# First modulations in fp32 on four column groups, and the Hyena filter steps moved into the opening, in a Trainium2 transformer block

## The chip, the cores and the metric

The kernel runs on one core of one Trainium2 chip. The time is that of one execution on the device, in microseconds. The kernel before took 2386.2 us, the median of three runs (2375.78 to 2389.0 us). The profile that is read here is of one more execution, of 2394.28 us.

## What is computed

One block of a diffusion model: 256 latent tokens and 256 context tokens of 2048 channels. The parts that the change touches are the first modulation and the Hyena filters.

```python
mod_c = silu(c_ctx) @ w_ada[:, :2 * D] + b_ada[:2 * D]      # context: shift, scale
mod   = silu(c) @ w_ada + b_ada                             # latents: six parts
parts = modulate(x, shift, scale) @ w_in                    # x * (1 + scale) + shift
hid = sin(sin(feats @ w1 + b1) @ w2 + b2)                   # 256 x 64
h   = (hid @ w3).reshape(L, 2, 2, 1024) * window            # taps: order, direction, channel
kf  = rfft(concat(h_fwd, 0, h_bwd[:0:-1]), n=2 * L)         # spectra of the filters
```

The spectra depend on weights alone; the long convolutions use them in the Hyena branch, much later in the program.

## The kernel before

All large products are made of fp32r matmuls, one pass over the moving operand each, from operands that were split into a high and a low part: `split` casts the high part on ScalarE (L138) and subtracts on VectorE (L139), and three matmuls (high by high, low by high, high by low) make one product. A scheduler orders the instructions of each engine at build time by a modelled time line; each engine then runs its list in that order. A tile waits for a free buffer of its tag ("wraw", "k8" and so on), and a DMA of SP's queue that waits holds up those behind it.

**The opening** has four rounds, q = 0 to 3. Each makes 512 columns of the first two modulations (shift and scale, `part`) for both streams. The silu of the two conditioning vectors, high and low parts, stands in four columns, repeated 32 times over to 128 columns (`csw`). 2048 x 512 of `w_ada` come in as four loads of 1 MB (`load4`), each is split in two pieces of 128x1024 (`split_ring`), and for each of 16 blocks of 128 rows two matmuls of 128 columns by 512 run (L396 with the high part, L397 with the low part). `mod_columns` then copies four rows out of PSUM, turns them into columns by matmuls with `sel` (L374) and adds the bias. `modulated` transposes a block of the inputs (L171) and applies shift and scale (L365), and `keys` and `gates_in` multiply the result by columns of `w_in` (`cm_block`, L220 to L223). These steps stand in a list, `later`, and are interleaved with the matmuls of the next round. Two steps of the filter generator (its two sines, L257 to L265) are in that list as well.

**The value stage** follows in `dn_early`, after the queries: four blocks of `proj_cm_ctx`, each 192 fp32r matmuls, and after each block two steps of the filter generator (`next(filt)`), eight in all. A step loads a window and two weights, makes the taps with four fp32 matmuls of 64 rows (L281), multiplies and adds them on VectorE (L282 to L290), splits them, runs 30 fp32r matmuls of 256 columns for the transform (`dft_mm`, L237 to L239), and stores a spectrum. All of that is one piece of the program, and the transform of a step stands directly behind its taps.

PSUM is used as two tags of four banks; ring, pages ("k8", seven of 8 KB a partition) and slots are SBUF buffers.

Of the kernel before, what the change touches and what calls it, by code (L numbers as in the profile page):

```python
# [16 lines left out]
P = 128  # L17
D = 2048
# [62 lines left out]
def tile_block(ctx: ExitStack, tc: tile.TileContext, A: dict, out: bass.AP):  # L81
# [51 lines left out]
    def bc(ap, shape):  # L133
        return ap.to_broadcast(shape)
# [57 lines left out]
    def as_rows(ap):  # L192
# [13 lines left out]
    nc.vector.tensor_copy(out=csw.rearrange("p k (r c) -> p k r c", c=4),  # L206
                          in_=bc(cs4.bitcast(F32).unsqueeze(2), [P, KT, 32, 4]))
    sel = cst.tile([4, 2], F32, name="sel")
    tt_(out=sel, in0=ident[0:4, 0:2], in1=ident[0:4, 2:4], op=ADD)

# [30 lines left out]
    def filters():  # L241
# [27 lines left out]
        load_const("dft", 2, 512, dh, dl)  # L269
        for c4 in range(4):  # L270
            hf, cs = c4 // 2, slice(c4 * 256, (c4 + 1) * 256)
            hs = slice((c4 % 2) * 256, (c4 % 2 + 1) * 256)
            for o in range(2):
                win, w3a, w3b, ht = page("win", (2, 256), (256,), (256,), (2, 2, 256))
                dma(out=win, in_=A["window"][:, cs].rearrange("(k p) c -> p k c", p=P))
                for d, w3 in enumerate((w3a, w3b)):
                    c0 = (o * 2 + d) * W + c4 * 256
                    dma(out=w3[:64, :], in_=A["hy_filt_w3"][0][:, c0:c0 + 256])
                    ps = sc_ps()
                    for i in range(2):  # L280
                        mm(ps[:, i * 256:(i + 1) * 256], hid[:, i * P:(i + 1) * P], w3[:64, :], start=True, stop=True)  # L281
                    tt_(out=ht[:, d], in0=ps.rearrange("p (i c) -> p i c", i=2), in1=win, op=MUL)  # L282
                hf_, hb_ = ht[:, 0], ht[:, 1]
                sk = slot([1, 256], "k1", "sk")
                dma(out=sk, in_=A["hy_skip"][0][o:o + 1, cs])
                tt_(out=hf_[0:1, 0, :], in0=hf_[0:1, 0, :], in1=sk, op=ADD)
                nc.vector.memset(hb_[0:1, 0, :], 0.0)
                smdf, sp = page("smdf", (2, 2, 256), (4, 256))
                tt_(out=smdf[:, 0], in0=hf_, in1=hb_, op=ADD)
                tt_(out=smdf[:, 1], in0=hf_, in1=hb_, op=SUB)  # L290
                h_, l_ = page("shl", (2, 2, 256), (2, 2, 256), dt=F32R)
                split(smdf, h_, l_)
                for i2 in range(2):
                    ps = sc_ps()
                    for i in range(2):
                        dft_mm(ps[:, i * 256:(i + 1) * 256], dh, dl, 2 * i2 + i, h_[:, i2], l_[:, i2])
                    copy(out=sp[:, 2 * i2:2 * i2 + 2, :].rearrange("p a c -> p (a c)"), in_=ps)
                ps = sc_ps()
                dft_mm(ps[:, 0:256], dh, dl, 2, h_[:, 0], l_[:, 0])
                ny = slot([1, 256], "k1", "ny")  # L300
                copy(out=ny, in_=ps[0:1, 0:256])
                nc.vector.memset(sp[0:1, 2, :], 0.0)
                dma(out=spec[o][hf][:, :, hs], in_=sp)
                dma(out=nyq[o][hf][:, hs], in_=ny)
                yield

# [7 lines left out]
    x_in, c_in = A["x"][0], A["ctx"][0]  # L314
    ring = slot([P, 4, 1024], "m16", "ring", F32R)
    turn = [0]
    raws = {}

    def load4(ap, k0, c0):
        raw = page("raw", (4, 512))  # L320
        nc.sync.dma_start(out=raw, in_=ap[k0 * P:(k0 + 4) * P, c0:c0 + 512].rearrange("(k p) c -> p k c", p=P))
        return raw

    def split_ring(raw):

        n = turn[0]
        turn[0] += 1
        hi = ring[:, n % 4].rearrange("p (k c) -> p k c", k=2)
        lo = slot([P, 2, 512], ("whi", "wlo")[n % 2], "wlo", F32R)
        split(raw, hi, lo)  # L330
        return hi, lo

# [4 lines left out]
    def gates_in(k0):  # L337
        raw, wh, wl = [slot([P, 4, P], "wraw", "wg", t) for t in (F32, F32R, F32R)]
        nc.sync.dma_start(out=raw, in_=w_in[k0 * P:(k0 + 4) * P, C_AB:C_AB + P].rearrange("(k p) c -> p k c", p=P))
        split(raw, wh, wl)  # L340
        for k in range(4):
            kt = k0 + k
            cm_block(pga, wh, wl, 0, k, [(slice(0, T), uxh[:, kt, :], uxl[:, kt, :]),
                                         (slice(T, 2 * T), uch[:, kt, :], ucl[:, kt, :])], kt == 0, kt == KT - 1)

    def keys(k0):
        if k0 % 4 == 0:
            raws["k"] = load4(w_in, k0, C_DK)
        wh, wl = split_ring(raws["k"][:, k0 % 4:k0 % 4 + 2, :])
# [19 lines left out]
    def mod_columns(mod, part, pmod, q):  # L369

        row = slot([4, 512], "k2", "modrow")
        copy(out=row, in_=pmod[0:4, :])
        for cc in range(4):
# [5 lines left out]

    later = []  # L380
    for q in range(4):
# [6 lines left out]
        for part in range(2):  # L388
            pmod = sc_ps()
            for kb in range(8):  # L390
                if kb % 2 == 0:
                    raw = load4(w_ada, kb * 2, part * D + q * 512)
                wh, wl = split_ring(raw[:, (kb % 2) * 2:(kb % 2) * 2 + 2, :])
                for k in range(2):
                    kt = kb * 2 + k
                    mm(pmod, csw[:, kt, :], wh[:, k, :], start=(kt == 0), stop=False)  # L396
                    mm(pmod, csw[:, kt, :], wl[:, k, :], start=False, stop=(kt == KT - 1))  # L397
                if later and (part * 8 + kb) % 2 == 1:
                    later.pop(0)()
            later.insert(0, lambda mod=mod, part=part, pmod=pmod, q=q: mod_columns(mod, part, pmod, q))  # L400
        for cc in range(4):
# [247 lines left out]
    def dn_early():  # L649
# [41 lines left out]
        for blk in range(4):  # L691
            pss = proj_cm_ctx(C_DV + blk * 256)
            for ch in range(2):
# [854 lines left out]
```

## Time and profile before

| what | value |
|---|---|
| median of three runs | 2386.2 us |
| the profiled execution | 2394.28 us |
| its span | 2392.6 us |
| TensorE busy | 2296.5 us, 96% |
| VectorE, ScalarE, GpSimd busy | 68%, 44%, 7% |
| mean granted TensorE clock | 0.986 of 2.4 GHz |
| DMA | 510.97 MB, 214 GB/s over the span |

The profiler shows one execution: for each engine the instructions with their start and duration, and what ended the idle time ahead of them. A matmul's record holds its way through the array, so records of a dense stream overlap; how fast the stream runs is read from the distance of two starts. Rates of the clock are shares of full speed (1.00 is 2.4 GHz, 0.5 is 1.2 GHz).

### The profile page before, as it was taken

To read this page: it belongs to the slowest core of one execution; us is meant where nothing else is said; L and a number is where in the kernel's file an instruction comes from. 1 tells how busy PE (TensorE), PEld (TensorE's weight loads), DVE (VectorE), ACT (ScalarE), POOL (GpSimd) and SP (SyncE) were. 2 spreads that over 40 slices of the span, in tenths; PEclk is the share of its full clock that TensorE was granted. 3 is DMA by queue.
4 is the path that set the end of the run, shared out by engine and by line. 5 is a ranking of instruction groups with operands and counts; after the bars stand their busy time and mean duration, and the time that the engine had idled before them with its cause. 6 is when DMAs were issued, how large, how long until landed. Compare 5 with 4: busy or idle time off the path is not lost.

```text
span 2392.6 us, 37188 instructions
## 1 busy us (share of the span) xinstructions
PE 2296.5 (96%) x14769; PEld 2073.8 (87%) x14769; DVE 1623.4 (68%) x2135; ACT 1052.1 (44%) x1417; POOL 175.0 (7%) x290
## 2 busy tenths in 40 slices
PE   6999898999999999899999999998999999999998
PEld 4889898889899999887888878888978987988986
DVE  6776467877788898976566656666655655555557
ACT  6665434434333433535443444444434433443442
POOL 0000221100200000121110021000000000000000
PEclk9999999999999999999999999999999999999999
DMA  9957767777663323499776797674667777656664
GB/s 324 330 188 256 221 184 239 244 254 240 201 176 96 109 89 107 137 245 276 228 233 215 257 319 254 235 239 129 217 215 231 255 229 231 184 193 224 192 202 149
DMA packets 295851, 510.97 MB, mean 214 GB/s; under 512 B 17414, under 2 KB 155105, under 8 KB 293084
## 3 DMA queue, kind: packets, MB, share of 16 engines
q1 hardware_dynamic: 271488, 422.63, 55.3%
q0 software_dynamic: 21408, 81.48, 10.8%
q10 hardware_dynamic: 2780, 4.47, 0.5%
q8 instruction: 116, 1.90, 0.3%
q14 instruction: 59, 0.48, 0.1%
HBM read 474.07 MB, written 34.45 MB: 213 GB/s over the span
## 4 chain that ended last, share of the span: by engine, by line
PE 68%; DMA 7%; DVE 5%; issue 3%; ACT 1%; POOL 0%; DVEq 0%; SPq 0%; ACTq 0%; POOLq 0%
PE mm L223 8%; PE mm L221 8%; PE mm L220 8%; PE mm L482 7%; PE mm L483 7%; PE mm L481 7%; DMA aw<-in_w_ada_dram 4%; PE mm L807 4%; PE mm L808 3%; PE mm L806 3%; DVE wlo L139 2%; PE ps L1037 1%; PE mm L941 1%; PE mm L942 1%; PE mm L939 1%
## 5 line engine op out<-in xcount | busy, mean ns | idle before, releaser
L138 ACT CAST whi<-wraw 128x1024 fp32r<-128x1024 f32 x584 | 612.9, 1051 | 965.4 <-PE mm L221 271.2
L139 DVE TENSOR_TENSOR wlo<-wraw,whi 128x1024 fp32r<-128x1024 f32 x584 | 708.5, 1221 | 337.7 <-PE mm L223 97.0
L523 DVE SCALAR_TENSOR_TENSOR acc<-aw,csil,acc 128x1024 f32<-128x1024 f32 x120 | 153.8, 1282 | 216.7 <-DMA aw<-in_w_ada_dram 216.4
L223 PE MATMUL mm<-uxh,wlo 128*128 128x256 f32 x1024 | 294.0, 288 | 3.6 <-DVE wlo L139 3.5
L223 PE MATMUL mm<-u2h,wlo 128*128 128x256 f32 x1024 | 291.0, 284 | 0.9 <-DVE wlo L139 0.8
L220 PE MATMUL mm<-u2h,whi 128*128 128x256 f32 x1024 | 290.8, 284 | 0.6 <-ACT u2h L138 0.6
L221 PE MATMUL mm<-u2l,whi 128*128 128x256 f32 x1024 | 290.8, 284 | 0.1
L220 PE MATMUL mm<-uxh,whi 128*128 128x256 f32 x960 | 276.0, 288 | 11.2 <-DVE cy L497 11.2
L221 PE MATMUL mm<-uxl,whi 128*128 128x256 f32 x960 | 275.9, 287 | 0.0
L223 PEld LDWEIGHTS mm<-uxh,wlo 128*128 128x128 f32 x1024 | 199.5, 195 | 5.5 <-DVE wlo L139 4.7
L482 PE MATMUL mm<-wlo,h 128*128 128x512 f32 x480 | 188.4, 393 | 13.7 <-DVE wlo L139 13.5
L223 PEld LDWEIGHTS mm<-u2h,wlo 128*128 128x128 f32 x1024 | 197.4, 193 | 1.3 <-DVE wlo L139 1.3
L220 PEld LDWEIGHTS mm<-u2h,whi 128*128 128x128 f32 x1024 | 197.5, 193 | 1.1 <-ACT u2h L138 1.0
L221 PEld LDWEIGHTS mm<-u2l,whi 128*128 128x128 f32 x1024 | 197.4, 193 | 0.6 <-DVE u2l L139 0.4
L220 PEld LDWEIGHTS mm<-uxh,whi 128*128 128x128 f32 x960 | 187.2, 195 | 11.9 <-issue 11.2
L221 PEld LDWEIGHTS mm<-uxl,whi 128*128 128x128 f32 x960 | 187.1, 195 | 2.0 <-issue 2.0
L483 PE MATMUL mm<-whi,h 128*128 128x512 f32 x480 | 187.4, 390 | 0.0
L481 PE MATMUL mm<-whi,h 128*128 128x512 f32 x480 | 186.9, 391 | 0.0
L807 PE MATMUL mm<-wlo,uxh 128*128 128x512 f32 x384 | 152.7, 398 | 6.1 <-DVE wlo L139 6.1
L808 PE MATMUL mm<-whi,uxl 128*128 128x512 f32 x384 | 152.1, 396 | 0.0
L806 PE MATMUL mm<-whi,uxh 128*128 128x512 f32 x384 | 150.0, 400 | 0.6 <-ACT whi L138 0.6
L223 PE MATMUL mm<-uch,wlo 128*128 128x256 f32 x448 | 127.9, 287 | 0.0
(541 smaller groups left out, 4681.9 us busy)
## 6 DMA issues: line engine op xcount, KB each, us to landing
wraw<-in_w_in_dram SPq DMA_DIRECT2D x264, 512.0 KB, 4.7
wraw<-in_w_ff_dram SPq DMA_DIRECT2D x256, 512.0 KB, 4.0
aw<-in_w_ada_dram SPq DMA_DIRECT2D x128, 512.0 KB, 4.6
raw<-in_w_ada_dram SPq DMA_DIRECT2D x32, 1024.0 KB, 7.9
wraw<-in_w_branch_dram SPq DMA_DIRECT2D x48, 512.0 KB, 5.1
wraw<-in_w_out_dram SPq DMA_DIRECT2D x32, 512.0 KB, 4.4
g_d<-gate POOLq DMA_DIRECT2D x24, 256.0 KB, 4.7
gatel<-g_d POOLq DMA_DIRECT2D x24, 256.0 KB, 5.6
```

The source lines that it names most:

```text
L138: copy(out=hi, in_=src)
L139: tt_(out=lo, in0=src, in1=hi.bitcast(F32), op=SUB)
L220: mm(ps[:, sl], wh[:, k, cs], ah, start=first and i == 0, stop=False, skip_group_check=True)
L221: mm(ps[:, sl], wh[:, k, cs], al, start=False, stop=False, skip_group_check=True)
L223: mm(ps[:, sl], wl[:, k, cs], ah, start=False, stop=last, skip_group_check=True)
L481: mm(pss[i], a, wh[:, k, :], start=(kt == 0), stop=False)
L482: mm(pss[i], a, wl[:, k, :], start=False, stop=False)
L483: mm(pss[i], b, wh[:, k, :], start=False, stop=(kt == nk - 1))
L523: stt(out=acc, in0=a, scalar=csil[:, 0, kt:kt + 1], in1=acc, op0=MUL, op1=ADD)
L806: mm(pg[i], a, wh[:, k, :], start=(kt == 0), stop=False)
L807: mm(pg[i], a, wl[:, k, :], start=False, stop=False)
L808: mm(pg[i], c, wh[:, k, :], start=False, stop=(kt == KT - 1))
```

## The change

1. The modulations are no longer split. `cs32` holds the silu of the two vectors in fp32, in the first two of 32 columns, the other 30 are zero. For each load of 1 MB four fp32 matmuls run, one for each of its four row blocks, each with 32 stationary columns and its own 32 partitions of one PSUM bank (L403). The column matmuls with `sel` then add the four groups, over 128 rows in place of four.
2. `ring` holds two raw loads in place of four high parts; `keys` and `gates_in` load through the same `wload` as all later products.
3. The filter generator has a step for its loads, one for its taps and one for its transform; one call to `next(filt)` runs the loads of step n + 1, the transform of step n - 1 and the taps of step n. Buffers of other tags are used for them.
4. All eleven calls are in the opening: five in the first round, two in each of the other three. The eight calls of the value stage are gone, and those of the sines too.

```diff
-    cs4 = slot([P, KT, 4], "k1", "cs4", F32R)
-    split(csil.rearrange("p a k -> p k a"), cs4[:, :, 0:2], cs4[:, :, 2:4])
-    csw = page("csw", (KT, P), dt=F32R)
...
+    cs32 = slot([P, KT, 32], "k4", "cs32")
+    nc.vector.memset(cs32, 0.0)
+    nc.vector.tensor_copy(out=cs32[:, :, 0:2], in_=csil.rearrange("p a k -> p k a"))
...
+        which = [(c4, o) for c4 in range(4) for o in range(2)]
+        got, made = loads(*which[0]), None
+        for n in range(len(which) + 1):
+            ahead = loads(*which[n + 1]) if n + 1 < len(which) else None
+            if made is not None:
+                spectrum(*which[n - 1], *made)
+            made = taps(*got) if got is not None else None
+            got = ahead
+            yield
...
-    ring = slot([P, 4, 1024], "m16", "ring", F32R)
+    ring = slot([P, 2, 4, 512], "m16", "ring")
...
+    later = [lambda: next(filt) for _ in range(5)]
...
-            for kb in range(8):
-                if kb % 2 == 0:
-                    raw = load4(w_ada, kb * 2, part * D + q * 512)
-                wh, wl = split_ring(raw[:, (kb % 2) * 2:(kb % 2) * 2 + 2, :])
-                for k in range(2):
-                    kt = kb * 2 + k
-                    mm(pmod, csw[:, kt, :], wh[:, k, :], start=(kt == 0), stop=False)
-                    mm(pmod, csw[:, kt, :], wl[:, k, :], start=False, stop=(kt == KT - 1))
-                if later and (part * 8 + kb) % 2 == 1:
+            for kb in range(4):
+                raw = load_ada(4 * kb, part * D + q * 512)
+                for j in range(4):
+                    mm(pmod[32 * j:32 * j + 32, :], cs32[:, 4 * kb + j, :], raw[:, j, :],
+                       start=(kb == 0), stop=(kb == 3))
+                for _ in range(-(-len(later) // (8 - 4 * part - kb))):
                     later.pop(0)()
...
-        if q in (1, 2):
-            later.append(lambda: next(filt))
+        if q < 3:
+            later += [lambda: next(filt) for _ in range(2)]
...
-            next(filt)
-            next(filt)
```

**How the orders move.** TensorE at the program's start, first before and then in the change (`ps` is a PSUM bank, `ring` and `wlo` are the high and low parts before, `ring` and `raw` the raw loads in the change):

```order
L171 MATMUL ps_75<-idon,colA_rows_68 128x128
L396 MATMUL ps_112<-ring_102,csw_83 128x512
L397 MATMUL ps_112<-wlo_115,csw_83 128x512
L396 MATMUL ps_112<-ring_102,csw_83 128x512
L397 MATMUL ps_112<-wlo_115,csw_83 128x512
```

```order
L171 MATMUL ps_75<-idon,colA_rows_68 128x128
L403 MATMUL ps_112<-ring_102,cs_3_80 32x512 x4
L258 MATMUL ps_127<-fT_118,w_18_120 64x256
L403 MATMUL ps_112<-raw_139,cs_3_80 32x512 x4
L403 MATMUL ps_112<-ring_102,cs_3_80 32x512 x4
L258 MATMUL ps_145<-z_129,w_19_122 64x256
L288 MATMUL ps_182<-w_30_168,z_147 128x256 x2
L288 MATMUL ps_186<-w_30_168,z_147 128x256 x2
L238 MATMUL ps_212<-shl_195,dfts_162 128x256
L238 MATMUL ps_226<-shl_195,dfts_162 128x256
```

Thirty-two matmuls of 512 columns for one modulation of a round became sixteen, in groups of four; three groups, the two sines and the first taps now stand ahead of the first transform, and the fourth group behind it.

TensorE in the value stage, before, around the taps of the third filter step (`vy` and `mm` belong to the values, `win` to the taps, `shl` and `dfts` to the transform), and in the change around the same transposes of values:

```order
L237 MATMUL ps_2442<-shl_2411,dfts_2387 128x256
L238 MATMUL ps_2442<-shl_2411,dfts_2387 128x256
L239 MATMUL ps_2442<-shl_2411,dfts_2387 128x256
L281 MATMUL ps_2457<-win_2454,z_1273 128x256 x2
L223 MATMUL mm_2902<-uch_100,wlo_3083 128x256
L220 MATMUL mm_2902<-uxh_98,whi_3082 128x256
```

```order
L222 MATMUL mm_2592<-ucl_101,whi_2713 128x256
L171 MATMUL ps_2584<-idon,vy_2576 128x128 x4
L224 MATMUL mm_2592<-uxh_98,wlo_2714 128x256
L224 MATMUL mm_2592<-uch_100,wlo_2714 128x256
L221 MATMUL mm_2592<-uxh_98,whi_2713 128x256
```

Only products and transposes of the values are left there; the 240 transform matmuls and 32 tap matmuls all stand in the opening.

SP's queue in the opening of the change (`wraw` are the loads for the keys and the gates):

```order
L342 DMA ring_102<-in_w_ada_dram 128x4x512 x2
L342 DMA raw_139<-in_w_ada_dram 128x4x512
L342 DMA ring_102<-in_w_ada_dram 128x4x512 x2
L342 DMA raw_198<-in_w_ada_dram 128x4x512
L342 DMA ring_102<-in_w_ada_dram 128x4x512
L143 DMA wraw_447<-in_w_in_dram 128x2x512
L143 DMA wraw_514<-in_w_in_dram 128x2x512
L143 DMA wraw_574<-in_w_in_dram 128x4x128
L342 DMA ring_102<-in_w_ada_dram 128x4x512
```

Seven loads of `w_ada` precede the first keys' weights; before, fifteen did, and the keys' weights went into pages. The keys' loads now share the four "wraw" buffers with the taps (`ht`).

## Rows read from the trace of the kernel before

**Rows 1.** The page: span, and TensorE's busy time, share, instructions.

```profile
span 2392.6 us, 37188 instructions
PE 2296.5 (96%) x14769; PEld 2073.8 (87%) x14769; DVE 1623.4 (68%) x2135; ACT 1052.1 (44%) x1417; POOL 175.0 (7%) x290
```

**Rows 2.** By stretch: length, busy PE, PEld, DVE, ACT, POOL; clock, DMA, GB/s.

```profile
0.00:166.20 166.20, 146.02 (x871) 123.25 (x871) 112.81 (x158) 108.13 (x159) 6.31 (x15) 0.97 0.81 284
166.20:270.00 103.80, 96.83 (x779) 95.72 (x778) 66.45 (x120) 62.11 (x139) 14.73 (x22) 0.95 0.81 260
270.00:422.00 152.00, 137.60 (x1028) 130.41 (x1029) 97.47 (x142) 60.06 (x82) 31.11 (x50) 0.96 0.65 199
```

**Rows 3.** Timeline of TensorE: the last matmul of the opening (start, duration).

```profile
165.87 0.28 PE L223 MATMUL ps<-uxh,wg 128*128 128x256 f32 x1
```

**Rows 4.** Groups in 0 to 166.2: busy us, mean ns, idle before, releasers.

```profile
L139 DVE TENSOR_TENSOR wlo<-raw,ring 128x1024 fp32r<-128x1024 f32 x72 | 85.5, 1220 | 26.2 <-ACT ring L138 25.9
L138 ACT CAST ring<-raw 128x1024 fp32r<-128x1024 f32 x72 | 72.2, 1047 | 27.1 <-DMA raw<-in_w_ada_dram 19.8 <-PE ps L396 3.9 <-PE mm L221 3.2
L397 PE MATMUL ps<-wlo,csw 128*128 128x512 f32 x128 | 54.9, 431 | 5.3 <-DVE wlo L139 5.3
L396 PE MATMUL ps<-ring,csw 128*128 128x512 f32 x128 | 53.2, 418 | 7.6 <-ACT ring L138 7.6
L220 PE MATMUL mm<-uxh,ring 128*128 128x256 f32 x64 | 17.1, 287 | 0.0
L171 PE MATMUL ps<-idon,xt 128*128 128x128 f32 x64 | 10.2, 300 | 0.0
```

**Rows 5.** Timeline of TensorE: two modulation matmuls in a dense stretch.

```profile
15.22 0.39 PE L397 MATMUL ps<-wlo,csw 128*128 128x512 f32 x1
15.45 0.40 PE L396 MATMUL ps<-ring,csw 128*128 128x512 f32 x1
```

**Rows 6.** Timeline of TensorE around the filter's first fp32 matmul (two records).

```profile
112.00 0.39 PE L396 MATMUL ps<-ring,csw 128*128 128x512 f32 x1
112.32 0.64 PE L257 MATMUL ps<-fT,w 33*64 33x256 f32 x2
112.89 0.39 PE L220 MATMUL mm<-uxh,ring 128*128 128x256 f32 x1
113.11 0.28 PE L221 MATMUL mm<-uxl,ring 128*128 128x256 f32 x1
113.23 0.28 PE L220 MATMUL mm<-uch,ring 128*128 128x256 f32 x1
```

**Rows 7.** Timeline of TensorE: taps of the first filter step, and what follows.

```profile
282.60 1.99 PE L281 MATMUL ps<-win,z 64*128 64x256 f32 x8
284.52 0.38 PE L220 MATMUL mm<-uxh,whi 128*128 128x256 f32 x1
```

**Rows 8.** Groups in 270 to 440: the filter steps on TensorE, VectorE and ScalarE.

```profile
L238 PE MATMUL ps<-shl,dfts 128*128 128x256 f32 x80 | 22.1, 284 | 0.0
L281 PE MATMUL ps<-win,z 64*128 64x256 f32 x64 | 17.0, 396 | 0.0
L282 DVE TENSOR_TENSOR win<-ps,win 128x512 f32<-128x512 f32 x16 | 10.9, 680 | 8.7 <-PE ps L281 8.6
L138 ACT CAST shl<-smdf 128x1024 fp32r<-128x1024 f32 x8 | 8.4, 1044 | 9.5 <-DVE smdf L290 9.5
L289 DVE TENSOR_TENSOR smdf<-win 128x512 f32<-128x512 f32 x8 | 5.5, 684 | 0.1
```

**Rows 9.** Timeline of TensorE: its longest wait in the value stage.

```profile
409.97 1.01 PE L237 MATMUL ps<-shl,dfts 128*128 128x256 f32 x3 [4.74 <-ACT shl L138]
```

**Rows 10.** By stretch of 20 us, columns as in rows 2: the opening's clock.

```profile
0.00:20.00 20.00, 6.82 (x18) 4.35 (x18) 8.65 (x14) 10.23 (x12) 2.52 (x8) 1.00 0.90 313
20.00:40.00 20.00, 15.85 (x55) 10.01 (x55) 13.05 (x13) 10.72 (x12) 0.00 (x0) 0.88 1.05 387
40.00:60.00 20.00, 17.15 (x70) 12.57 (x70) 15.62 (x20) 18.04 (x30) 0.00 (x0) 0.86 0.79 273
```

**Rows 11.** DMA in 0 to 166.2: bytes moved, and their rate.

```profile
DMA packets 25929, 47.19 MB, mean 284 GB/s; under 512 B 1285, under 2 KB 4830, under 8 KB 25917
```

**Rows 12.** Groups in 0 to 166.2: the sine chain, applying a modulation.

```profile
L263 DVE SCALAR_TENSOR_TENSOR z<-z,z 64x256 f32<-64x256 f32 x6 | 2.5, 416 | 0.1
L365 ACT ACTIVATE uf<-ps,mod 128x256 f32<-128x256 f32 x32 | 16.0, 557 | 11.2 <-PE ps L171 6.0 <-DVE mod L378 3.6 <-DVE wlo L139 1.6
```

More of the change, by code (lines that the diff above doesn't have):

```diff
@@ L201, in tile_block @@
     act(out=csil.rearrange("p a k -> p (a k)"), in_=colA[:, 0:32], func=AF.Silu)
-    cs4 = slot([P, KT, 4], "k1", "cs4", F32R)
-    split(csil.rearrange("p a k -> p k a"), cs4[:, :, 0:2], cs4[:, :, 2:4])
-    csw = page("csw", (KT, P), dt=F32R)
[L206 to L209, printed above, removed]
+    cs32 = slot([P, KT, 32], "k4", "cs32")
+    nc.vector.memset(cs32, 0.0)
+    nc.vector.tensor_copy(out=cs32[:, :, 0:2], in_=csil.rearrange("p a k -> p k a"))
+    sel = cst.tile([P, 2], F32, name="sel")
+    tt_(out=sel, in0=ident[:, 0:2], in1=ident[:, 32:34], op=ADD)
+    for j in (2, 3):
+        tt_(out=sel, in0=sel, in1=ident[:, 32 * j:32 * j + 2], op=ADD)
     eps = cst.tile([P, 2], F32, name="eps")
@@ L269, in filters @@
         load_const("dft", 2, 512, dh, dl)
[L270 to L297, printed above, removed]
-                ps = sc_ps()
[L299 to L305, printed above, removed]
@@ new lines, in loads @@
+        def loads(c4, o):
+            cs = slice(c4 * 256, (c4 + 1) * 256)
+            win, w3 = slot([P, 2, 256], "k2", "win"), slot([64, 2, 256], "k2", "w3")
+            dma(out=win, in_=A["window"][:, cs].rearrange("(k p) c -> p k c", p=P))
+            for d in range(2):
+                c0 = (o * 2 + d) * W + c4 * 256
+                dma(out=w3[:, d, :], in_=A["hy_filt_w3"][0][:, c0:c0 + 256])
+            sk = slot([1, 256], "k1", "sk")
+            dma(out=sk, in_=A["hy_skip"][0][o:o + 1, cs])
+            return win, w3, sk
@@ new lines, in taps @@
+        def taps(win, w3, sk):
+            ht = slot([P, 2, 2, 256], "wraw", "ht")
+            for d in range(2):
+                ps = sc_ps()
+                for i in range(2):
+                    mm(ps[:, i * 256:(i + 1) * 256], hid[:, i * P:(i + 1) * P], w3[:, d, :], start=True, stop=True)
+                tt_(out=ht[:, d], in0=ps.rearrange("p (i c) -> p i c", i=2), in1=win, op=MUL)
+            hf_, hb_ = ht[:, 0], ht[:, 1]
+            tt_(out=hf_[0:1, 0, :], in0=hf_[0:1, 0, :], in1=sk, op=ADD)
+            nc.vector.memset(hb_[0:1, 0, :], 0.0)
+            smdf = slot([P, 2, 2, 256], "wlo", "smdf")
+            tt_(out=smdf[:, 0], in0=hf_, in1=hb_, op=ADD)
+            tt_(out=smdf[:, 1], in0=hf_, in1=hb_, op=SUB)
+            h_, l_ = page("shl", (2, 2, 256), (2, 2, 256), dt=F32R)
+            split(smdf, h_, l_)
+            return h_, l_
@@ new lines, in spectrum @@
+        def spectrum(c4, o, h_, l_):
+            hf, hs = c4 // 2, slice((c4 % 2) * 256, (c4 % 2 + 1) * 256)
+            sp = slot([P, 4, 256], "whi", "sp")
+            for i2 in range(2):
+                ps = sc_ps()
+                for i in range(2):
+                    dft_mm(ps[:, i * 256:(i + 1) * 256], dh, dl, 2 * i2 + i, h_[:, i2], l_[:, i2])
+                copy(out=sp[:, 2 * i2:2 * i2 + 2, :].rearrange("p a c -> p (a c)"), in_=ps)
+            ps = sc_ps()
+            dft_mm(ps[:, 0:256], dh, dl, 2, h_[:, 0], l_[:, 0])
+            ny = slot([1, 256], "k1", "ny")
+            copy(out=ny, in_=ps[0:1, 0:256])
+            nc.vector.memset(sp[0:1, 2, :], 0.0)
+            dma(out=spec[o][hf][:, :, hs], in_=sp)
+            dma(out=nyq[o][hf][:, hs], in_=ny)
@@ L314, in tile_block, with load_ada @@
     x_in, c_in = A["x"][0], A["ctx"][0]
-    ring = slot([P, 4, 1024], "m16", "ring", F32R)
+    ring = slot([P, 2, 4, 512], "m16", "ring")
     turn = [0]
[L317 to L324, printed above, removed]
+    def load_ada(k0, c0):
         n = turn[0]
         turn[0] += 1
[L328 to L331, printed above, removed]
+        raw = ring[:, n // 2 % 2] if n % 2 == 0 else page("raw", (4, 512))
+        nc.sync.dma_start(out=raw, in_=w_ada[k0 * P:(k0 + 4) * P, c0:c0 + 512].rearrange("(k p) c -> p k c", p=P))
+        return raw
     psk = [mm_ps() for _ in range(4)]
@@ L337, in gates_in @@
     def gates_in(k0):
-        raw, wh, wl = [slot([P, 4, P], "wraw", "wg", t) for t in (F32, F32R, F32R)]
-        nc.sync.dma_start(out=raw, in_=w_in[k0 * P:(k0 + 4) * P, C_AB:C_AB + P].rearrange("(k p) c -> p k c", p=P))
-        split(raw, wh, wl)
+        wh, wl = wload(w_in, k0, 4, C_AB, P)
         for k in range(4):
@@ L346, in keys @@
     def keys(k0):
[L347 to L349 removed]
+        wh, wl = wload(w_in, k0, 2, C_DK, 512)
         for k in range(2):
@@ L369, in mod_columns @@
     def mod_columns(mod, part, pmod, q):
-        row = slot([4, 512], "k2", "modrow")
-        copy(out=row, in_=pmod[0:4, :])
+        row = slot([P, 512], "k2", "modrow")
+        copy(out=row, in_=pmod)
         for cc in range(4):
```

5 lines of the change are left out of this document (3 added, 2 removed).

## The prediction, made before the changed kernel ran

> **What bounds the kernel now.** The page comes first: TensorE is busy for 96% of the span [rows 1], so a change is worth what it takes from TensorE's work or from its waits. The stretches come second [rows 2]: up to 166.2 us, where the opening's last matmul ends [rows 3], TensorE is busy for 146.0 us; from 270 to 422 us, where most filter steps run, for 137.6 of 152.0 us. The groups of the opening come third [rows 4]. The reader should see there that all 72 modulation and key pieces pass ScalarE (1.05 us each) and VectorE (1.22 us each), and that the modulation matmuls wait for both: 7.6 us behind ScalarE, 5.3 us behind VectorE; ScalarE in turn waits 19.8 us for the loads.
>
> A matmul's record overlaps the next one's, so I count TensorE's work by the distance of starts. A modulation matmul takes 0.23 us [rows 5], an fp32r matmul of 256 columns 0.12 us (113.11 to 113.23) [rows 6]. The opening holds 256 modulation matmuls (59 us), 480 of 256 columns for keys and gates (six groups of 64 like the one in [rows 4], and 96; 58 us), and 64 transposes and 64 column records, some 0.12 us each (15 us), with 1 us for the sines: 133 us. So 33 of the 166 us are waits, most of them in the first 60 us, where TensorE is busy for 6.8, 15.9 and 17.2 of each 20 us, and the clock falls to 0.88 and 0.86, a mixture of 1.2 and 2.4 GHz [rows 10].
>
> **What is removed.** The 256 modulation matmuls: -59 us. With them go 64 of the 72 splits on each of ScalarE and VectorE, 67 and 78 us, which cost TensorE only through the waits above.
>
> **What is added: 32 groups of four fp32 matmuls.** The trace of before has no fp32 matmul of 512 columns. Its nearest row is that of the taps: 256 columns, 64 records for 32 matmuls, so two records each [rows 8], and eight of them run from 282.60 to 284.52 us, 0.24 us a record [rows 7]. The sine's matmul shows what a change of the array's tile costs: it starts 0.32 us after the one before, in place of 0.23, its two records take 0.57 in place of 0.48, and the next starts 0.22 after the first product, in place of 0.12 [rows 6]; together about 0.3 us. A record of 512 columns is then 0.45 us (a little under twice 0.24, of which a few hundredths are fixed). The price of a group hangs on one thing: whether four matmuls that use different 32 columns of the array run beside each other.
> - All four at once: 2 x 0.45 + 0.3 = 1.2 us, 32 groups 38 us.
> - One after the other: 8 x 0.45 + 0.3 = 3.9 us, 32 groups 125 us.
>
> No row shows two tiles of the array at work at a time. I take the lower end. The dense streams show that the engine starts a matmul while the one before is still on its way (0.39 us records 0.23 us apart [rows 5]); what spaces them is the stream of columns through the same part of the array, and the four of a group share no column, no operand and no part of PSUM. That is an inference, so the other end keeps a large chance below. The Trainium skill, "TensorEngine Tiling (Array Packing)", Key Properties, says that tiles operate independently and that different ones can execute in parallel; no run here shows it yet.
>
> **What is moved: eight filter steps.** A step has four tap matmuls, 8 records at 0.24 us (1.9 us), and 30 transform matmuls at 0.12 us (3.6 us) [rows 6 to 8] (three groups of 80 like that of L238): 5.5 us, eight steps 44 us. The opening gets +44 us, the value stage -44 us. There the longest wait of TensorE, 4.74 us for a filter's split [rows 9], goes as well, -5 us: the transform stood directly behind its taps. The value stage then stays with TensorE: its DMA ran at 199 GB/s, where the opening reached 387 [rows 2, 10], and VectorE was busy for 97 of 152 us with filter work in it. POOL gets the steps' small loads and spectra in either place; the 47 MB that the opening moves [rows 11] grow by about 8 MB (windows 2, weights 1, spectra 4, constants 1), and 55 MB at 387 GB/s are 143 us, less than the opening will need.
>
> **The opening's waits.** Now 33 us. In the change:
> - before the first matmul: the first load is no longer behind two loads of gate weights and needs no split, about 8 us;
> - the first filter step: sine, sine, taps, split, transform follow each other, and the transform stands in TensorE's list ahead of the fourth group. A sine takes six VectorE operations of about 0.4 us [rows 12] and one on ScalarE, some 3.5 us; taps to transform takes four operations of 0.68 us and a cast of 1.04 us [rows 8], with small ones and both matmul ends about 6 us. From 8 to about 25 us TensorE has three groups (3.6), sines (1) and taps (2): 11 us of waits. The second step has one group, the column matmuls and its own taps in 7 us: 3 us;
> - in each round, from the second modulation to the first product: column matmuls, the bias, two operations of 0.56 us on ScalarE [rows 12] and a split, about 3 us, four times 12 us.
>
> That makes 34 us, as much as now, so this is 0 in the sum. The same early gaps let the clock fall, as they do now. SP's queue holds three loads for the keys behind the taps' buffers, and w_ada loads behind those; seven loads are in or ahead by then, and I price that at nothing; if it isn't covered, it costs up to 10 us in the first round.
>
> **Sum.** Opening: -59 + 38 + 44 + 0 = +23 us (it ends near 190 us). Value stage: -44 - 5 = -49 us. Together -26 us, taken as -25 for the column matmuls, now over 128 rows in place of four. Later work is not touched: the program goes by counts of loads, not by time. The profiled execution, 2394.3 us, would be 2369 us; the median of the runs lies 8 us lower, so I predict 2386.2 - 25 = 2361 us. Its own range: groups between 0.9 (no tile cost) and 1.5 us, -10 to +10; waits 10 either way; the value stage between -44 and -54: 2345 to 2374 us.
>
> **Rivals.**
> - *In pairs.* Each fp32 matmul is two records on the same columns. If matmuls start in the order of the program, as all starts in the trace do, the second half of one keeps the next one's first half waiting until the first half is through, and only neighbours overlap: 5 x 0.45 + 0.3 = 2.55 us for a group that stands alone, 77 us for 32 with some side by side. Opening: -59 + 77 + 44, less some 4 us of waits that the longer groups fill: +58; value stage -49; +9 us, 2395 us. For it: the order of starts; against it: nothing in the rows. The Trainium skill, "TensorE: Matmul & The Clock Gate", The mechanism, states just this order: matmuls are strict FIFO in start and in end. The trace agrees as to starts.
> - *One after the other* (slower). The tiles don't overlap at all in fp32: 125 us. Opening -59 + 125 + 44 - 5 = +105, value stage -49: +56 us, 2442 us. It decides from about 2.0 us a group on, where the sum passes zero. For it: the 64-column sine matmul took no less per record than the 128-column taps (0.57 for two against 0.24 each), so fewer columns alone save nothing.
> - *The value stage gives back half.* Its time could be held by loads and VectorE once the filters are gone, as in the 4.74 us wait's neighbourhood: -25 in place of -49, 2385 us. Against it: the DMA rate and VectorE's share above.
> - *The steps don't fill waits.* That is already in the sum: I credit nothing for filling.
>
> **How the numbers follow.** About 0.5%, 12 us, is what a measurement of this kernel can tell from no change. At once 0.50, pairs 0.27, one after the other 0.15, half back 0.08. Faster by over 12 us: nearly all of the first (0.48) and a little of the others, 0.50. Slower: 0.15 and a third of the pairs, 0.25. The same: 0.25. The range reaches from 2342 us to the upper part of the pairs' own spread, 2408 us; outside lie the 0.15 of the serial case and a few hundredths at the ends.
>
> **What would show it.** Right: a group of L403 whose eight records start in about 0.9 us; no ring splits on ScalarE and VectorE in the opening; last gate product near 190 us; no L281-like or transform matmul after it; the stretch from there to the end of the values shorter by about 49 us. Pairs: starts of the records 0.45 us apart with two under way. Wrong altogether: eight starts over 3.6 us, or waits of TensorE in the opening well over 34 us, for the first taps' window loads on POOL's queue or for w_ada.

## The result, and the profile after

The changed kernel takes 2426.4 us (median of 4 runs, 2415.9 to 2429.7); the kernel before took 2381.0 us beside it. The ratio is 1.0174, 95% interval 1.0152 to 1.0196: slower by 1.7%, where 2361 us, 1% faster, was forecast. The page of after, its first lines, against [rows 1]:

```profile
span 2425.0 us, 37041 instructions
PE 2284.1 (94%) x14769; PEld 2041.3 (84%) x14769; DVE 1552.8 (64%) x2073; ACT 991.5 (41%) x1353; POOL 173.9 (7%) x290
```

TensorE is busy for 12 us less, VectorE for 71 and ScalarE for 61, and the span is 32 us longer. By stretches (columns as in [rows 2]): one of 20 us, then the opening's first 80 us, the rest of it, and all of it.

```profile
20.00:40.00 20.00, 7.89 (x28) 4.89 (x21) 7.20 (x14) 1.46 (x2) 5.81 (x10) 0.60 0.52 164
0.00:80.00 80.00, 40.27 (x200) 22.32 (x201) 25.75 (x54) 15.47 (x25) 16.47 (x32) 0.80 0.73 254
80.00:243.90 163.90, 141.11 (x976) 111.09 (x975) 53.90 (x102) 50.11 (x100) 17.88 (x30) 0.89 0.67 224
0.00:243.90 243.90, 181.39 (x1174) 133.41 (x1175) 79.65 (x155) 65.58 (x124) 34.35 (x62) 0.86 0.69 234
```

From 20 to 40 us TensorE works 7.9 us, where it worked 15.9 [rows 10], at a clock of 0.60, and the DMA moves 164 GB/s in place of 387. VectorE and ScalarE are idle for two thirds of the opening: neither bounds it any more. The timeline of TensorE of after shows where the opening ends (to compare with [rows 3]), and what follows:

```profile
243.86 0.29 PE L224 MATMUL ps<-uch,wlo 128*128 128x256 f32 x1
250.07 0.63 PE L593 MATMUL ps<-idon,gT 32*128 32x32 f32 x4 [5.82 <-ACT gT L590]
259.39 0.55 PE L221 MATMUL mm<-uxh,whi 128*128 128x256 f32 x1 [8.69 <-DVE cy L506]
```

The opening ends at 243.9 us instead of 165.9, 78 us later; near 190 had been forecast. To follow the loss further I take one mark that all kernels share, the first gate matmul behind the values and the filters (L806 before, L813 after). A line's matmuls, with the first and last start:

```profile
L806 PE MATMUL mm<-whi,uxh x384: 387/389/629, 449.1 to 1332.0; 128*128 128x512 f32 x192
```
```profile
L813 PE MATMUL mm<-whi,uxh x384: 387/389/628, 475.7 to 1368.1; 128*128 128x512 f32 x192
```

From the opening's end to this mark it is 283.2 us before and 231.8 after: 51 us less. So in these two executions the opening lost 78 us, the value stage gave back 51, and the rest is 6 us longer. Those 6 us say nothing: from the mark to the end the fourteen kernels below take 1939 to 1950 us, in no order that follows the edits. TensorE's waits of after from 0 to 262 us, the seven largest (who waited, for whom: us in total, times, longest):

```profile
PE ps L238 <- ACT shl L138: 16.4, 5, 3.8
PE ps L403 <- DMA raw<-in_w_ada_dram: 13.3, 3, 8.9
PE ps L171 <- DMA colA_rows<-in_b_ada_dram: 9.8, 1, 9.8
PE mm L221 <- DVE cy L506: 8.7, 1, 8.7
PE ps L288 <- DMA w<-in_hy_filt_w_dram: 8.3, 1, 8.3
PE ps L171 <- ACT uf L373: 5.8, 5, 2.4
PE ps L593 <- ACT gT L590: 5.8, 1, 5.8
```

### The profile page after: what moved, and what is told of

Read it like the earlier page. It is cut to its first block, busy times and chain, and to the rows that moved or that the text cites. A ratio compares the mean times of both kernels' runs of the same rounds, so it can differ in the third digit from the quotient of the medians.

```text
span 2425.0 us, 37041 instructions
## 1 busy us (share of the span) xinstructions
PE 2284.1 (94%) x14769; PEld 2041.3 (84%) x14769; DVE 1552.8 (64%) x2073; ACT 991.5 (41%) x1353; POOL 173.9 (7%) x290
## 4 chain that ended last, share of the span: by engine, by line
PE 70%; DMA 14%; DVE 9%; issue 4%; ACT 3%; POOL 0%; DVEq 0%; ACTq 0%; SPq 0%; POOLq 0%
PE mm L224 10%; PE mm L222 10%; PE mm L221 10%; DMA aw<-in_w_ada_dram 9%; PE mm L491 6%; PE mm L492 6%; PE mm L490 6%; DVE wlo L139 3%; PE mm L814 3%; PE mm L815 3%; PE mm L813 3%; DMA wraw<-in_w_in_dram 2%; PE ps L403 1%; DVE acc L532 1%; DMA raw<-in_w_ada_dram 1%
## 5 line engine op out<-in xcount | busy, mean ns | idle before, releaser
L138 ACT CAST whi<-wraw 128x1024 fp32r<-128x1024 f32 x596 | 623.0, 1048 | 949.2 <-PE mm L222 265.6
L139 DVE TENSOR_TENSOR wlo<-wraw,whi 128x1024 fp32r<-128x1024 f32 x596 | 720.5, 1217 | 346.8 <-PE mm L224 90.9
L221 PE MATMUL mm<-uxh,whi 128*128 128x256 f32 x1024 | 290.8, 287 | 8.7 <-DVE cy L506 8.7
L222 PE MATMUL mm<-uxl,whi 128*128 128x256 f32 x1024 | 292.3, 286 | 0.7 <-DVE uxl L139 0.7
L221 PEld LDWEIGHTS mm<-uxh,whi 128*128 128x128 f32 x1024 | 197.0, 194 | 12.0 <-issue 10.5
L222 PEld LDWEIGHTS mm<-uxl,whi 128*128 128x128 f32 x1024 | 198.3, 194 | 2.7 <-DVE uxl L139 1.8
L813 PE MATMUL mm<-whi,uxh 128*128 128x512 f32 x384 | 150.7, 402 | 1.1 <-ACT whi L138 1.1
```

Of the source, the lines that this page charges most:

```text
L138: copy(out=hi, in_=src)
L139: tt_(out=lo, in0=src, in1=hi.bitcast(F32), op=SUB)
L221: mm(ps[:, sl], wh[:, k, cs], ah, start=first and i == 0, stop=False, skip_group_check=True)
L222: mm(ps[:, sl], wh[:, k, cs], al, start=False, stop=False, skip_group_check=True)
L813: mm(pg[i], a, wh[:, k, :], start=(kt == 0), stop=False)
```

## The experiments

"The change" is the changed kernel, 2426 us. "Opening" and "mark" are the opening's last matmul and the mark above, in the profiled execution. Each ratio goes by the kernel before as it ran beside that kernel. Intervals are some 0.4% wide, so two kernels that lie less than 8 us apart are hardly told apart.

| kernel | us, median | ratio to before, 95% | opening | mark |
|---|---|---|---|---|
| before | 2381 to 2384 | 1 | 165.9 | 449.1 |
| the change | 2426.4 | 1.0174 (1.0152 to 1.0196) | 243.9 | 475.7 |
| e1 groups alone | 2379.0 | 0.9978 (0.9959 to 0.9996) | 165.1 | 431.6 |
| e2 filter steps alone | 2455.5 | 1.0309 (1.0283 to 1.0336) | 286.1 | 511.4 |
| e3 loads ahead | 2418.6 | 1.0148 (1.0125 to 1.0171) | 245.9 | 477.5 |
| e4 calls apart | 2387.0 | 1.0018 (0.9998 to 1.0037) | 220.2 | 441.8 |
| e5 ht elsewhere | 2423.6 | 1.0167 (1.0144 to 1.0191) | 249.7 | 480.7 |
| e6 one call early | 2407.8 | 1.0089 (1.0058 to 1.0120) | 242.4 | 469.6 |
| e7 e1, half bytes | 2363.1 | 0.9914 (0.9889 to 0.9938) | 148.6 | 416.8 |
| e8 later rounds | 2422.0 | 1.0158 (1.0136 to 1.0181) | 248.7 | 476.4 |
| e9 e4 with e3 | 2401.1 | 1.0072 (1.0044 to 1.0100) | 233.6 | 452.0 |
| e10 e1, rows first | 2378.1 | 0.9968 (0.9953 to 0.9984) | 164.2 | 430.1 |
| e11 change, half bytes | 2414.2 | 1.0112 (1.0080 to 1.0144) | 229.6 | 464.0 |
| e12 e2, calls apart | 2445.0 | 1.0250 (1.0211 to 1.0288) | 286.1 | 498.7 |

**e1: the column groups alone.** The filters as before, undivided and in the value stage; of its edits, the calls in the opening, against the change:

```diff
-    later = [lambda: next(filt) for _ in range(5)]
+    later = []
...
-        if q < 3:
-            later += [lambda: next(filt) for _ in range(2)]
+        if q in (1, 2):
+            later.append(lambda: next(filt))
```

> The fp32 column groups alone; the filter steps stay in the value stage, undivided, as before the change. Theory W (the opening's loss is made of waits that the filter steps bring in: their loads, their splits, and the weight loads that then stand behind the groups' buffers): no filter step is in the opening, so it loses the 59 us of the old modulations and pays 38 us, and ends near 145 us instead of 165.9; the value stage is as before; time about 2360 to 2365 us. Rival G (the fp32 groups hold the weights' buffers until TensorE has read them, where a split freed them early, and the loads fall behind with or without filter steps): the opening ends at 166 to 190 us, time 2381 to 2405 us.

Theory W falls here: the opening has some 27 us less work and ends where it did. Stretches of e1:

```profile
20.00:40.00 20.00, 7.46 (x40) 2.35 (x40) 1.41 (x5) 3.14 (x4) 0.00 (x0) 0.82 1.06 382
40.00:60.00 20.00, 13.03 (x68) 4.67 (x68) 1.11 (x4) 4.41 (x11) 0.00 (x0) 0.67 1.05 386
```

TensorE is idle for half of these 40 us while the DMA moves as many GB/s as it did at its best before. The removed work had lain beside the loads. The Trainium skill, "DMA: Bandwidth & Descriptors", Specifications, gives a core about 358 GB/s from HBM, half of a stack's 716; the trace, with one core at work, shows 382 and 386 over 20 us each, and the measurement decides.

**e2: the filter steps alone.** The old modulations and the divided `filters`, none of it left in the value stage, and `later` taken as fast as the change takes it:

```diff
-                if later and (part * 8 + kb) % 2 == 1:
-                    later.pop(0)()
+                if kb % 2 == 1:
+                    for _ in range(-(-len(later) // (8 - 4 * part - kb // 2))):
+                        later.pop(0)()
```

> The divided filter steps in the opening alone; the modulations are the old fp32r ones with split weights. Theory W: the opening takes 166 us, 44 us of filter work and nearly all of the waits that the change brought (some 50 us), the value stage gives back its 46 to 49 us: 2415 to 2430 us. Rival G: the filter steps bring only the waits of their own chains (8.5 us at the first taps, 4.5 at the first transform, three times 4.8 at the second call of a round, some 28 us), not those on the weights: about 2395 to 2405 us.

2455 us, above both. Waits of e2 from 0 to 286 us:

```profile
PE ps L414 <- ACT ring L138: 23.7, 8, 5.1
PE ps L237 <- ACT shl L138: 14.4, 4, 3.8
```

The old modulations wait for their casts three times as long as before (7.6 us [rows 4]). ScalarE's list now holds the steps' casts too, for which it waits 29.5 us, and its wait for the modulations' loads grew from 19.8 us [rows 4] to 27.4; what share each has wasn't tried apart. So the two halves of the change are not a sum: the groups are worth 3 us without filter steps (e1) and 29 with them (2455 to 2426).

**e3: the filter loads ahead.** The skip rows out of the small buffers that TensorE frees, and a call between the first loads and the first taps:

```diff
-            sk = slot([1, 256], "k1", "sk")
+            sk = k4[0:1, 512 + 256 * o:768 + 256 * o]
...
         got, made = loads(*which[0]), None
+        yield
...
-    later = [lambda: next(filt) for _ in range(5)]
+    later = [lambda: next(filt) for _ in range(6)]
```

> The changed kernel with the filters' skip rows in a free half of another buffer, so that no filter load waits in the DMA queue for a small buffer that TensorE must free, and with the first filter loads a whole call ahead of the first taps. Theory W: the 8.5 us wait at 30 us goes and with it part of the 26 us in which the weight queue stood behind the groups' buffers: 10 to 25 us less than the changed kernel, 2401 to 2416 us. Rival G, and a rival by which the waits only move to the next late transfer: within 5 us of the changed kernel, 2421 to 2426 us.

8 us less than the change, between the two ranges and hardly clear of the noise. The 8.3 us wait for the filters' weights is gone, but the wait for the modulation's loads grows from 13.3 to 20.6 us (e3, 0 to 246 us):

```profile
PE ps L405 <- DMA raw<-in_w_ada_dram: 20.6, 3, 13.5
PE ps L239 <- ACT shl L138: 16.7, 5, 3.8
```

**e4: the two calls of a round apart.**

```diff
             later.append(lambda xt=xt, mod=mod, kt=4 * q + cc: modulated(xt, mod, kt))
+            if q < 3 and cc == 1:
+                later.append(lambda: next(filt))
...
             later.append(lambda k0=4 * q + 2 * kb: keys(k0))
+            if q < 3 and kb == 0:
+                later.append(lambda: next(filt))
...
-        if q < 3:
-            later += [lambda: next(filt) for _ in range(2)]
```

> The changed kernel with the two filter calls of a round two or more steps apart (after the second modulated block and after the first key block) instead of next to each other. Theory W: the second call's transform no longer waits for the split of the taps right ahead of it; three times 3.74 to 3.82 and 1.02 us go, 12 to 14 us: 2412 to 2414 us. Rival: the taps' split is late wherever the call stands, or the time is taken again by the next late weight load: 2421 to 2426 us.

39 us less than the change, three times what I expected. All waits of e4 over 1 us from 80 to 262 us:

```profile
PE mm L221 <- ACT whi L138: 3.7, 3, 1.7
PE ps L403 <- DMA raw<-in_w_ada_dram: 2.4, 4, 1.1
PE ps L288 <- DVE ht L289: 1.6, 2, 0.8
PE mm L221 <- DVE cy L508: 1.5, 1, 1.5
PE ps L595 <- ACT gT L592: 1.4, 1, 1.4
```

Against the same stretch of the change, the transforms' waits are gone, and those of the transposes for ScalarE (5.8 us) and the two at the front of the value stage (14.5 us, now 2.9). With the waits goes the low clock. Stretches of e4, to compare with those of the change above:

```profile
0.00:80.00 80.00, 40.45 (x209) 23.12 (x210) 22.75 (x50) 12.51 (x21) 17.74 (x34) 0.81 0.69 235
80.00:220.20 140.20, 129.07 (x967) 100.67 (x967) 59.64 (x115) 57.32 (x111) 17.78 (x30) 0.99 0.81 277
```

Nothing changes in the first 80 us. From there to the opening's end TensorE is idle for 11 us in place of 23, and the clock is 0.99 in place of 0.89. Of the 39 us, 24 are won in the opening and 10 between its end and the mark; the rest lies behind the mark, within the spread of that part.

**e5: the taps' buffer.**

```diff
-            ht = slot([P, 2, 2, 256], "wraw", "ht")
+            ht = slot([P, 2, 2, 256], "whi", "ht")
```

> The changed kernel with the taps' product (ht) in another group of buffers than the weight loads' (wraw). In the changed kernel the weight queue stands 18.2 us at the end of the opening, until the last taps give back such a buffer, and the value stage's first loads stand behind it. Theory Q (the lateness of the second filter call hurts because it holds the weight queue): the opening's end and the first waits of the value stage shrink, 15 to 25 us less than the changed kernel, 2401 to 2411 us. Rival S (the stall of TensorE between two calls that stand next to each other, with the half clock after it, is the cost itself): within 6 us of the changed kernel, 2420 to 2427 us.

No gain, as rival S had it; but Q isn't excluded, for the queue of the weights (SP) then stood for another buffer in 195 to 275 us of e5, 27.7 us at a stretch:

```profile
SPq L519 <- DVE wlo L139: 34.3, 4, 27.7
```

**e6: only the first call early.** The second stays at the round's end:

```diff
             later.append(lambda xt=xt, mod=mod, kt=4 * q + cc: modulated(xt, mod, kt))
+            if q < 3 and cc == 1:
+                later.append(lambda: next(filt))
...
         if q < 3:
-            later += [lambda: next(filt) for _ in range(2)]
+            later.append(lambda: next(filt))
```

> The changed kernel with only the first filter call of a round moved, to behind the second modulated block; the second stays where it was, at the end of the round, and is no longer next to the other. Theory Q (the second call's late place holds the weight queue): most of the 39 us that setting both calls apart gave stays lost, 2412 to 2422 us. Rival S (the stall between adjacent calls and the half clock after it): about all of it comes back, 2385 to 2395 us.

2408 us, below Q's range and above S's: each of the two moves is worth some 20 us. The first call's taps now stand one group and eight transposes ahead of the second call's transform, and this is no lead: TensorE of e6, 0 to 262 us.

```profile
PE ps L238 <- ACT shl L138: 15.3, 6, 3.6
```

**e7: e1 with half the bytes.** Each load brings two of its four blocks, and the groups read those twice, so the modulations are of half the weights:

```diff
-        nc.sync.dma_start(out=raw, in_=w_ada[k0 * P:(k0 + 4) * P, c0:c0 + 512].rearrange("(k p) c -> p k c", p=P))
+        nc.sync.dma_start(out=raw[:, 0:2], in_=w_ada[k0 * P:(k0 + 2) * P, c0:c0 + 512].rearrange("(k p) c -> p k c", p=P))
...
-                    mm(pmod[32 * j:32 * j + 32, :], cs32[:, 4 * kb + j, :], raw[:, j, :],
+                    mm(pmod[32 * j:32 * j + 32, :], cs32[:, 4 * kb + j, :], raw[:, j % 2, :],
```

> The column groups alone, as in the first of these kernels, but each modulation load brings half of its 1 MB, and each half of the groups reads the same two blocks (the modulations are then of half the weights). Theory B (without filter steps the opening is bound by the weights' transfer, 380 GB/s from 20 to 120 us, not by TensorE): the opening ends 20 to 30 us earlier, near 140 us, and the time is 2350 to 2362 us. Rival G (the wait is for buffers that TensorE frees late, not for bytes): the opening ends within 8 us of where it did, 2370 to 2380 us.

The opening ends 16.5 us earlier and the time falls by 16: nearer to theory B than to G, though short of B's size. No instruction of TensorE was taken away for this. The queue of the weights waits for buffers that groups free for 34.4 us in e1 and 33.9 in e7, so it isn't that wait which got shorter. **e10** asks the same from the other side: the small rows of `colA` go to the weights' queue, ahead of all but one load.

```diff
-    def rows_to_cols(specs, name):
+    def rows_to_cols(specs, name, q=nc.scalar):
...
-            nc.scalar.dma_start(out=rt[r:r + n, :], in_=ap)
+            q.dma_start(out=rt[r:r + n, :], in_=ap)
...
-        (as_rows(b_ada[0:2 * D]), 32), (as_rows(b_ada[3 * D:5 * D]), 32)], "colA")
+        (as_rows(b_ada[0:2 * D]), 32), (as_rows(b_ada[3 * D:5 * D]), 32)], "colA", nc.sync)
```

> The column groups alone (2379 us), with the small rows that the silu needs issued on the queue of the weights, ahead of all but one 1 MB load. Theory B (the opening without filter steps is bound by the transfer of the weights): the first group starts some 10 us earlier, at 12 to 15 us instead of 23.6, and the time stays within 4 us, 2375 to 2383 us. Rival (the late start is carried to the end): 8 to 12 us less, 2367 to 2371 us.

The first group of e1 and of e10, in the timeline of TensorE:

```profile
23.61 1.93 PE L385 MATMUL ps<-ring,cs 128*32 128x512 f32 x8 [10.51 <-DVE cs L205]
```
```profile
13.87 1.94 PE L385 MATMUL ps<-ring,cs 128*32 128x512 f32 x8 [2.36 <-DVE cs L205]
```

Ten us earlier at the start, one at the opening's end, as theory B has it. **e11** halves the loads' bytes in the change itself, by the edit of e7.

> The changed kernel, but each modulation load brings half of its 1 MB, and each half of the groups reads the same two blocks (the modulations are then of half the weights). Theory C (the 44 us over the forecast are waits that the order of TensorE's instructions makes: transforms behind their taps, transposes behind their copies, the first waits of the value stage): at most the waits for modulation loads go, some 10 of 17 us: 2412 to 2422 us. Theory B (the transfer of the weights bounds this opening too): 20 us or more go, 2395 to 2406 us.

12 us less, as theory C has it: the wait for the modulation's loads falls from 13.3 to 4.2 us, and most of the rest stands. Waits of e11, 0 to 240 us:

```profile
PE ps L238 <- ACT shl L138: 17.0, 5, 3.7
PE ps L593 <- ACT gT L590: 6.8, 1, 6.8
PE ps L288 <- DMA w<-in_hy_filt_w_dram: 5.7, 1, 5.7
PE ps L403 <- DMA raw<-in_w_ada_dram: 4.2, 1, 4.2
```

**e8: the steps in the later rounds.** e4 with e3's loads; the sines and first loads alone in the first round, then three calls a round (the diff is against e4 with e3's edits):

```diff
-    later = [lambda: next(filt) for _ in range(6)]
+    later = [lambda: next(filt) for _ in range(3)]
...
         later.append(lambda k0=4 * q: gates_in(k0))
+        if q < 3:
+            later.insert(1, lambda: next(filt))
```

> The kernel with the calls apart, further with only the sines and the first filter loads in the first round, three calls in each later round, and the skip rows out of the small buffers' way. Theory W (waits of the first round, 33 us in 20 to 80 us, are made by filter steps whose loads are late): the first round runs at the loads' rate and 15 to 25 us go: 2362 to 2372 us, faster than before the change. Rival B (the weights' transfer bounds the opening's start whatever stands between the groups): within 8 us of the kernel with the calls apart, 2379 to 2395 us.

Both missed: 35 us slower than e4. With three calls in a round, taps and transform stand close again, and the keys wait for their weights (12.0 us, 3.7 in e4). TensorE of e8, 0 to 262 us:

```profile
PE ps L239 <- ACT shl L138: 14.6, 6, 2.9
PE mm L222 <- ACT whi L138: 12.0, 5, 7.2
```

**e9: the edits of e3 and e4 together.**

> The kernel with the two calls of a round apart (2387 us), further with the first filter loads a call ahead of the first taps and the skip rows out of the small buffers' way. Theory W: the 8.5 us that TensorE waits for the filters' weights near 30 us, and the 3.6 us for the first transform's split, go and nothing takes their place: 2374 to 2380 us. Rival M (the first round's lost time moves to the next late modulation load, as it did in the kernel with the loads ahead alone): within 5 us of it, 2382 to 2392 us.

Both missed again: 14 us slower than e4. The 8.5 us wait for the filters' weights is gone, but the first transform's wait isn't, the modulations wait longer for their loads (15.5 us in e4), and the keys much longer for the split of their weights (3.7 us in e4). TensorE of e9, 0 to 262 us, and its longest wait for a load:

```profile
PE ps L405 <- DMA raw<-in_w_ada_dram: 19.0, 4, 11.3
PE mm L222 <- ACT whi L138: 14.6, 5, 5.7
```
```profile
74.98 1.08 PE L405 MATMUL ps<-raw,cs 128*32 128x512 f32 x4 [11.30 <-DMA raw<-in_w_ada_dram]
```

The queue of the weights stands 23.6 us at a stretch for a half of the ring that a group has still to read, but in e4 it stands 26.2, so that isn't what e9 lost. Rival M was right in kind and too small; why the keys' weights came late wasn't tried.

**e12: e2 with the calls apart,** the edit of e4.

> The old fp32r modulations with the divided filter steps in the opening (2455 us), the two calls of a round apart. Its transform still stands only some transposes and one modulation step behind the taps. If setting calls apart is worth as much here as in the changed kernel (39 us), 2411 to 2421 us; if the distance behind the taps decides and not the calls' places, little is won: 2440 to 2455 us. Beside the same order with column groups (2387 us) it tells what the groups are worth once filter steps stand in the opening: by their work alone 21 us, by their freed VectorE and ScalarE more.

10 us: the second case's range, but not its reason. The transform's wait falls from 14.4 to 3.6 us, so the calls' places do decide it here too; the modulations' wait for their casts grows from 23.7 to 30.6 us, and the opening ends where it did. TensorE of e12, 0 to 286 us:

```profile
PE ps L414 <- ACT ring L138: 30.6, 10, 4.8
PE ps L237 <- ACT shl L138: 3.6, 1, 3.6
```

Beside e4 the groups are worth 58 us.

No version with filter steps in the opening beats the kernel before; e4 can't be told from it. e10, the groups alone with the rows first, is 0.16 to 0.47% faster than it, and 48 us faster than the change.

## Why the prediction was wrong, step by step

**What was removed, and the price of a group: right.** Eight records of a group in the timeline of TensorE of after, at the full clock:

```profile
42.78 1.06 PE L403 MATMUL ps<-raw,cs 128*32 128x512 f32 x8
43.77 0.38 PE L239 MATMUL ps<-shl,dfts 128*128 128x256 f32 x1
```

The next matmul starts 0.99 us after the group's start; "all four at once" had said 1.2. One after the other would be 3.9, in pairs 2.55. Both rivals that rested on the price are out. The chances were spread over this price, and no case but the first, with 10 us either way, asked about the waits. The Trainium skill, "TensorE: Matmul & The Clock Gate", The mechanism and Measured speedup vs the span model, gives a pack of tiles one matmul's time and a few ns for each further tile; the 0.99 us agree to a tenth of a us, and the strict order of starts and ends, from which I had made the pairs, held nothing up.

**The value stage: the direction right, the size unclear to some 15 us.** 51 us against 49 forecast in the two profiled executions; that it is so close is partly luck, for e1, e7 and e10, with the undivided steps there, need 266 to 268 us from the opening's end to the mark, where the profiled execution of before, 12 us above its median, took 283. Against them the change saves 35, and e4, without the two waits at the front of the stage, 45. The rival "the value stage gives back half" didn't come true.

**The opening's waits: the step that failed.** "That makes 34 us, as much as now, so this is 0 in the sum." At full clock the work is 133 - 59 + 32 x 0.99 + 44 = 150 us (156 forecast); the opening is 244 us, so 94 us are waits and low clock, 60 more than I allowed. TensorE was busy for 181.4 of the 244 us, so some 62 us are idle time and, by estimate, 31 us (181 less 150) are work that ran slower than at full clock; in e4 the same count gives 51 and 20. Of the 33 us that I called waits in the kernel before, TensorE was idle for 20 (166.2 less 146.0); the other 13 are, by the same estimate, slow work. Waits well over 34 us were the sign that I had named for "wrong altogether"; of the 62, though, only 22 are for the first taps' loads and for `w_ada`, which I had named with it. The parts, as they were put:
- The first filter step, put at 11 us of waits, with its loads taken for landed. They weren't. On POOL's queue a skip row waits 6.6 us for a buffer that the second sine's matmul frees, and the windows and tap weights stand behind it. The first call issues its own loads, so there was no step between loads and taps. TensorE, 28 to 40 us, of after:

```profile
29.94 3.75 PE L288 MATMUL ps<-w,z 64*128 64x256 f32 x8 [8.29 <-DMA w<-in_hy_filt_w_dram]
37.26 1.01 PE L238 MATMUL ps<-shl,dfts 128*128 128x256 f32 x3 [3.56 <-ACT shl L138]
38.90 0.41 PE L240 MATMUL ps<-shl,dfts 128*128 128x256 f32 x1
39.11 0.41 PE L238 MATMUL ps<-shl,dfts 128*128 128x256 f32 x1
```

- "SP's queue ... I price that at nothing; if it isn't covered, it costs up to 10 us in the first round." The place was right and the reason wrong: in the first round not the taps' buffers but the ring held it. The queue of after:

```profile
21.57 0.50 SPq L342 DMA_DIRECT2D raw<-in_w_ada_dram  x1
48.24 0.37 SPq L342 DMA_DIRECT2D ring<-in_w_ada_dram  x1
```

  26 us without a load, for a buffer that a group standing behind the filter work must free. TensorE then waits for weights:

```profile
69.20 1.93 PE L403 MATMUL ps<-raw,cs 128*32 128x512 f32 x8 [8.93 <-DMA raw<-in_w_ada_dram]
70.91 1.93 PE L403 MATMUL ps<-ring,cs 128*32 128x512 f32 x8
```

  Before, splits emptied the loads' buffers, and the queue's longest stand for one was 7.1 us; now TensorE alone frees them. How much of the time this costs isn't shown: in all, the queue stands 121 us for the groups in the change and 127 in e4, which is 39 us faster.
- The later rounds: I counted 12 us from modulation to product and nothing for the filter steps, since the code puts a step's transform one call behind its taps. But the two calls of a round stand next to each other, so one call's taps and the next one's transform have nothing between them. TensorE, 112 to 114 us, of after (again at 162 and 211 us):

```profile
112.23 0.79 PE L238 MATMUL ps<-shl,dfts 128*128 128x256 f32 x2 [3.57 <-ACT shl L138]
113.49 0.58 PE L239 MATMUL ps<-shl,dfts 128*128 128x256 f32 x1 [0.47 <-DVE shl L139]
```

  The 4.74 us wait that I credited to the value stage [rows 9] went to the opening and became five. e4 shows that these places, with what stands around them, cost 39 of the 65 us by which the change missed the forecast. The other 26 us aren't traced to a cause by a run: e4 is still idle for 40 of its first 80 us, and e3, e8 and e9, which aimed there, won 8 us at most.
- "The same early gaps let the clock fall, as they do now." It fell much further: a mean of 0.86 over 243.9 us is some 68 us at 1.2 GHz (0.14 is half the share of the time at the lower level), and the transforms above start 0.21 us apart instead of 0.12, at a granted clock of 0.50.

**Work taken from TensorE counted in full: wrong for the groups alone.** The sum put -59 + 38 at its whole size, though [rows 10] show 387 GB/s beside an idle TensorE. e1 and e7 together show that an opening without filter steps waits for the weights: 27 us of work less gave 3, 16.8 MB less gave 16. I had the 47.19 MB [rows 11] and used them only to ask whether the new opening would be long enough for its bytes, not whether the old one's end was set by them. In the change itself this isn't the loss: beside the filter steps the groups are worth 29 us (e2 against the change), more than the 21 of the sum.

**Open.** Why the calls' places also set the first waits of the value stage wasn't settled: e5 only moved the queue's wait to another buffer. What the low clock alone costs wasn't tried apart from the waits; the 31 us above are an estimate.

## What to carry to other kernels

Before work is taken from the engine that looks full, ask stage by stage what its idle time there waits for; where it is a load at the rate that the DMA reaches at its best, the work is hidden and its removal is worth little (3 us here, without the filter steps). A step moved in front brings its loads and its chain of splits along: look in the engine's order for what stands between the producer and its consumer, since a lead that is written in the code is worth only what the order leaves of it (39 us here for moving six calls by a few places, 10 with the old modulations). And where a conversion that emptied the load buffers is dropped, count how long the consumer now holds them, and what else stands in that consumer's list.

## What the runs showed of the hardware

- Four fp32 matmuls of 512 columns on four column groups, two records each, take 0.99 us at 2.4 GHz (42.78 to 43.77 above), hardly more than one alone by its price of 0.9 us; at a granted clock of 0.50 the same group takes 1.71 us, from 69.20 to the next group's start at 70.91 in the change.
- The work behind a wait ran at a lower clock: the granted clock was 0.60 from 20 to 40 us of after, where TensorE was busy for 7.9 us, and from 80 us to the opening's end 0.89 in the change, idle for 23 us there, and 0.99 in e4, idle for 11.
